# First two token tiles of the input projection taken singly, with the first weights loaded ahead of the second tile

## The chip, the cores and the metric

The kernel runs on one core of a Trainium2 chip. The metric is the device time of one execution in microseconds (us). Before the change it is 1400.34 us, the median of 3 runs (1399.54 to 1401.05).

## What is computed

One layer of an encoder on 1024 tokens of 1024 features, in float32: a norm, one wide input projection, two parallel branches, a merge, a feed-forward part and a final norm. The change touches the first lines of it alone:

```python
h = rmsnorm(x, norm_mix[l])          # x * rsqrt(mean(x*x) + EPS) * gain
proj = h @ w_in[l]
q, k, v, r, lr_f, lr_b, u, g_a, g_b = jnp.split(proj, split_points, axis=-1)
log_a_f = jax.nn.log_sigmoid(lr_f @ w_decay_up_fwd[l] + b_decay_fwd[l]) / GATE_NORMALIZER
...
o = o_fwd + o_bwd                    # gated linear attention, both directions, 4 heads
...
x = x + merged @ w_out[l]
x = x + (jax.nn.silu(gate) * up) @ w_ffn_out[l]
return rmsnorm(x, norm_final)
```

## The kernel before

**Numbers and tiles.** Every matrix product is made of three matmuls (`products`, line 288): each operand is split into a high part, rounded to the matmul's float32r format, and a low part, which is the rest. ScalarE (ACT in the profile) rounds, and VectorE (DVE) or GpSimd (POOL) subtracts. The tokens are cut into eight tiles of 128. `x` tiles arrive by DMA in four buffers that are used in turn, so that the load of tile t + 4 waits until tile t has been scaled (`load_x`, line 370; `norm_x`, line 393).

**The norm of one tile** (`norm_x`, lines 393 to 397, with lines 320 to 332) runs over three engines: ACT squares and sums the tile, DVE adds epsilon (the small `n1rs<-n1ms` row), POOL takes the power -1/2, and DVE multiplies the tile by it (`xn<-x,n1rs`). DVE takes its instructions in order, and so stands while POOL works on the power that its next instruction reads.

**The turn to features** (`to_features`, line 352). TensorE transposes the scaled tile into PSUM (`tr<-ident,xn`, line 338), ACT multiplies by the gain and rounds to the high part `hh` (line 345), and DVE makes the low part `hl` (line 348). Before the change this is always done for two token tiles at once: a PSUM bank holds two feature pieces of two token tiles, and an ACT or DVE instruction works on 128 partitions by 256 tokens.

**The first product** (`first_values`, line 415) multiplies one token tile by 288 columns: the 256 value columns of the first head and 32 columns of the low-rank decay inputs. It takes 8 features pieces of three matmuls each, 24 in all. The value columns come in four chunks of 256 KB (`raw`, line 206), the 32 decay columns in one small load (`lraw`, line 384). `FirstWeights` (line 236) splits them into `fwh` and `fwl`: the high part of a chunk on ACT, the low part of chunks 0 and 1 on DVE, of 2 and 3 on POOL; the decay columns wholly on POOL. When the sum of a token tile is done, ACT and DVE split it (`vh`, `vl`) and ACT copies the decay columns (`lr`, line 421), which on ACT stands behind the `vl` of DVE.

**The order of the work** is written out by hand: every engine executes what the program issues in the order in which it issues it. `begin` puts a generator on a side list, and `pump` (line 159), called after every three matmuls, takes its next step when a credit counted in matmul lengths has run out; `finish_side` runs what is left. In the first stage (lines 442 to 487) the order is: norm of tiles 0 and 1, their transposes, the split of all first weights, their gain and split, the norms of tiles 2 and 3, then pairs of token tiles; the norms of tiles t + 4 and t + 5 are begun ahead of tile t, the transposes for tiles t + 2 and t + 3 in the middle of tile t + 1.

Of the kernel before, what the change touches and what calls it, by code (L numbers as in the profile page):

```python
# [17 lines left out]
P = 128  # L18
# [34 lines left out]
def kernel(  # L53
# [146 lines left out]

    def load(src, kts, c0, width):
        per = min(HALF // width, kts)
        tiles = []
        for k0 in range(0, kts, per):
            raw = wts.tile([P, per, width], F32, tag="raw", name=name("raw"), bufs=4)
            nc.sync.dma_start(
                raw[:, :, :],
                src[k0 * P : (k0 + per) * P, c0 : c0 + width].rearrange("(k p) c -> p k c", p=P),
            )
            tiles.append(raw)  # L210
        return tiles

# [23 lines left out]
    class FirstWeights(Weights):  # L236
# [6 lines left out]

        def split_values(self, i, eng):
            split_to(*(t[:, :, :DV] for t in self.parts[i]), self.todo[i][:, :, :], eng)

# [81 lines left out]

    def norm_scale(xt, sq, s):
        ms = vec(1, s + "ms")  # L330
        nc.scalar.activation(sq[:, :], xt, AF.Square, scale=1.0 / 32.0, accum_out=ms[:, :])
        return rms_scale(ms[:, :], 1, s + "rs")

    def transpose_tile(ps, xt, i, kp):
# [16 lines left out]

    def to_features(xn, t0, act, gain):

        for kp in range(KT // 2):
            ps = bank(ps_g, "tr")
            for i in range(2):
                transpose_tile(ps, xn[i], i, kp)
            gain_and_split(ps, kp, t0, act, gain)
            yield 1

# [9 lines left out]
    def load_x(t):  # L370
        nc.sync.dma_start(xt[t % 4][:, :], x[t * P : (t + 1) * P, :])

    def load_rows(tile, at, v, n):
        nc.sync.dma_start(tile[at : at + n, :], v[0].rearrange("(j p) -> j p", p=P))
# [6 lines left out]
    load_rows(rows[0], 0, norm_mix, 8)  # L381
    load_x(1)
    first_raw = load(*next(order))
    nc.sync.dma_start(lraw[:, :, :], w_in[:, LR0:U0].rearrange("(k p) c -> p k c", p=P))
    for t in (2, 3):
        load_x(t)
# [5 lines left out]

    def norm_x(t):
        rs = norm_scale(xt[t % 4][:, :], xn[t % 4], "n1")
        scale_by(xn[t % 4], xt[t % 4][:, :], rs)
        if t + 4 < NT:
            load_x(t + 4)

    def norms(t0):
# [15 lines left out]
    def first_values(w, v, t):  # L415

        ps = bank(ps_mm)
        for kt in range(KT):
            mm3(ps[:, :VL], tokens(hT(kt, t // 4), t), w(kt), kt == 0, kt == KT - 1)
        split_to(*(part[:, t % 4, :] for part in v[t // 4]), ps[:, :DV])  # L420
        nc.scalar.copy(low_rows[:, t, :, :], ps[:, DV:VL].unsqueeze(1).broadcast_to([P, 4, 2 * RANK]))
# [33 lines left out]
    b_dec = (cols[1][:, 24:28], cols[1][:, 28:32])  # L455
    norm_x(1)
    trs = [bank(ps_g, "tr") for _ in range(KT // 2)]
    for t in range(2):
        for kp, ps in enumerate(trs):
            transpose_tile(ps, xn[t], t, kp)  # L460
    w = FirstWeights(first_raw, lraw)
    w.split_low()
    for i in range(KT // 2):
        w.split_values(i, nc.vector if i < 2 else nc.gpsimd)
    for kp, ps in enumerate(trs):
        gain_and_split(ps, kp, 0, hT, g_mix)
    norm_x(2)
    norm_x(3)
    for t in range(0, NT, 2):
        if t + 4 < NT:  # L470
            begin(norms(t + 4), 1)
        if t == 2:
# [3 lines left out]
            fetch()  # L476
        first_values(w, v, t)
        finish_side()
        if t == 0:
            vectors(1, 8)  # L480
        if t + 2 < NT:
            begin(to_features(xn[(t + 2) % 4 :], t + 2, hT, g_mix), 0.5)
        first_values(w, v, t + 1)
        finish_side()
# [1393 lines left out]
```

## Time and profile before

| what | value |
|---|---|
| time of the runs | 1400.34 us median, 1399.54 to 1401.05 |
| time of the profiled execution | 1400.29 us, of it 1398.6 us span |
| TensorE busy | 1367.3 us (98% of the span) |
| VectorE, ScalarE, GpSimd busy | 848.1, 624.0, 751.1 us |
| TensorE busy in the first 32 us | 22.76 us |

The span runs from the first to the last instruction of the profiled execution; the rest of its time, 1.7 us, lies around it. A row of the timeline has start, duration, engine, line, operation and tiles, how many instructions were merged in it, and in brackets how long the engine had stood idle before it and what ended that. A matmul's own duration overlaps that of the next, so its pace is read from the distance of two starts. PE is TensorE; SPq is the queue that issues the loads. Buffer numbers are left out of names, so `xn<-x` is the norm of any token tile.

### The profile page before, as it was taken

The numbers are of one execution on the slowest core, as the hardware profiler recorded it, in microseconds if no ns is written. First come the engines' busy times: TensorE is split into PE (matmuls) and PEld (weight loads), VectorE is DVE, ScalarE is ACT, GpSimd is POOL, SyncE is SP. The second block draws the span as 40 slices with busy tenths as digits, with TensorE's granted clock in tenths as the row PEclk, the third lists the DMA queues.
The fourth block names the chain that finished last, engine by engine and source line by source line (L and its number), as shares of the span: only waits on it lengthen the run. The fifth ranks groups of instructions, "written<-read, shape, count | busy, mean of one in ns | idle before, by whom it ended". The sixth has DMA issues, their size and how long they took to land. (4 is left out here: it accounts for less than half of the span.)

```text
span 1398.6 us, 18511 instructions
## 1 busy us (share of the span) xinstructions
PE 1367.3 (98%) x6654; PEld 1152.5 (82%) x6654; DVE 848.1 (61%) x1073; ACT 624.0 (45%) x1125; POOL 751.1 (54%) x565
## 2 busy tenths in 40 slices
PE   7999999999999999899999999999999999999997
PEld 6889898988888888788887888888888888888876
DVE  6266757667745885587875865556565556343364
ACT  6364655554334444455346633333333334453253
POOL 3261716041387555468665176666666667464364
PEclk9999999999999999999999999999999999999999
DMA  6211423322477668997425455554444447976461
GB/s 191 76 57 50 136 64 103 106 62 75 135 241 234 207 215 270 323 402 275 151 76 183 164 180 173 173 173 159 147 140 148 142 153 254 385 257 216 165 240 62
DMA packets 167453, 243.56 MB, mean 174 GB/s; under 512 B 10905, under 2 KB 97857, under 8 KB 167361
## 3 DMA queue, kind: packets, MB, share of 16 engines
q1 hardware_dynamic: 154944, 216.16, 46.3%
q10 hardware_dynamic: 12416, 26.22, 5.0%
q8 instruction: 52, 0.85, 0.3%
q14 instruction: 41, 0.33, 0.1%
HBM read 164.48 MB, written 77.86 MB: 173 GB/s over the span
## 5 line engine op out<-in xcount | busy, mean ns | idle before, releaser
L199 POOL TENSOR_TENSOR wl<-fs,wh 128x512 fp32r<-128x512 f32 x120 | 165.0, 1379 | 163.9 <-ACT wh L198 141.3
L291 PE MATMUL ps<-gl,wh 128*128 128x512 f32 x616 | 240.0, 390 | 0.8 <-DVE gl L1472 0.8
L291 PE MATMUL ps<-gh,wh 128*128 128x512 f32 x616 | 240.6, 391 | 0.0
L291 PE MATMUL ps<-gh,wl 128*128 128x512 f32 x616 | 239.9, 390 | 0.0
L199 POOL TENSOR_TENSOR wl<-fraw,wh 128x512 fp32r<-128x512 f32 x90 | 129.9, 1443 | 67.2 <-ACT wh L198 66.5
L199 POOL TENSOR_TENSOR ol<-gor,oh 128x1024 fp32r<-128x1024 f32 (+1 forms) x42 | 102.1, 2437 | 91.9 <-ACT oh L198 72.9
L291 PE MATMUL ps<-hh,wh 128*128 128x512 f32 x376 | 149.5, 398 | 0.0
L291 PE MATMUL ps<-hh,wl 128*128 128x512 f32 x376 | 146.8, 391 | 0.0
L291 PE MATMUL ps<-hl,wh 128*128 128x512 f32 x376 | 146.6, 390 | 0.0
L291 PEld LDWEIGHTS ps<-gl,wh 128*128 128x128 f32 x616 | 115.7, 188 | 24.9 <-DVE gl L1472 1.3
L291 PEld LDWEIGHTS ps<-gh,wl 128*128 128x128 f32 x616 | 115.7, 188 | 24.2
L199 POOL TENSOR_TENSOR wl<-raw,wh 128x512 fp32r<-128x512 f32 x44 | 61.4, 1411 | 137.7 <-ACT wh L198 135.2
L291 PEld LDWEIGHTS ps<-gh,wh 128*128 128x128 f32 x616 | 115.7, 188 | 23.6
L291 PE MATMUL ps<-oh,oh 128*128 128x512 f32 x308 | 120.0, 390 | 1.3 <-DVE x L1800 1.3
L291 PE MATMUL ps<-ol,oh 128*128 128x512 f32 x308 | 120.1, 390 | 0.2 <-DVE ol L199 0.2
L291 PE MATMUL ps<-oh,ol 128*128 128x512 f32 x308 | 119.9, 389 | 0.0
L199 POOL TENSOR_TENSOR wl<-wraw,wh 128x512 fp32r<-128x512 f32 x56 | 90.7, 1646 | 46.7 <-ACT wh L198 46.7
L199 DVE TENSOR_TENSOR ol<-wor,oh 128x1024 fp32r<-128x1024 f32 (+1 forms) x42 | 63.9, 1542 | 53.1 <-ACT oh L198 50.0
L198 ACT CAST wh<-fs 128x512 fp32r<-128x512 f32 x120 | 73.8, 615 | 30.8 <-DVE fs L902 23.1
L291 PEld LDWEIGHTS ps<-hh,wl 128*128 128x128 f32 x376 | 70.6, 188 | 15.1
L291 PEld LDWEIGHTS ps<-hl,wh 128*128 128x128 f32 x376 | 70.7, 188 | 13.4
L291 PEld LDWEIGHTS ps<-hh,wh 128*128 128x128 f32 x376 | 70.7, 188 | 13.4
(258 smaller groups left out, 3173.2 us busy)
## 6 DMA issues: line engine op xcount, KB each, us to landing
fraw<-in_w_ffn_in_dram SPq DMA_DIRECT2D x44, 512.0 KB, 6.4
gor<-g_out SPq DMA_DIRECT2D x35, 512.0 KB, 7.0
raw<-in_w_in_dram SPq DMA_DIRECT2D x48, 256.0 KB, 4.4
g_out<-s SPq DMA_DIRECT2D x44, 256.0 KB, 2.3
fraw<-in_w_in_dram SPq DMA_DIRECT2D x20, 512.0 KB, 4.2
wor<-t_out SPq DMA_DIRECT2D x20, 512.0 KB, 7.6
g_out<-g SPq DMA_DIRECT2D x33, 256.0 KB, 2.6
x<-in_x_dram SPq DMA_DIRECT2D x16, 512.0 KB, 3.9
```

Of the source, the lines that this page charges most:

```text
L198: nc.scalar.copy(hi, src)
L199: eng.tensor_tensor(lo, src, as_f32(hi), op=ALU.subtract)
L291: nc.tensor.matmul(ps, a[i], b[j], start=first and n == 0, stop=last and n == 2, skip_group_check=onto)
```

## The change

Loads: the first two weight chunks, the decay columns and the last two chunks are now issued ahead of `x` tile 1. Before, tile 1 stood ahead of them and the decay columns behind all four chunks.

Token tiles 0 and 1 are each turned to features by themselves (`features_of`): a PSUM bank holds two feature pieces of one token tile, and the ACT and DVE instructions work on 128 by 128. TensorE multiplies token tile 0 before it transposes token tile 1. The squares, roots and scalings of tiles 1, 2 and 3 are put one by one between the pieces of tiles 0 and 1. The high part of weight chunk 2 stands behind the first two pieces of tile 0 and its low part goes to DVE; chunk 3 is split wholly on POOL.

Tiles 2 and 3 are still turned to features together, with 256-token instructions, but now amid the matmuls of token tile 1, three matmuls apart. The norms of tiles 4 and 5, which stood ahead of the split of token tile 0's sum, stand behind the features of tiles 2 and 3. From the matmuls of token tile 2 on, every engine has the same instructions in the same order as before.

```diff
-    load_x(1)
-    first_raw = load(*next(order))
-    nc.sync.dma_start(lraw[:, :, :], w_in[:, LR0:U0].rearrange("(k p) c -> p k c", p=P))
-    for t in (2, 3):
+    first_raw = load(*next(order), and_then={1: load_low})
+    for t in (1, 2, 3):
         load_x(t)
...
-        def split_values(self, i, eng):
-            split_to(*(t[:, :, :DV] for t in self.parts[i]), self.todo[i][:, :, :], eng)
+        def high(self, i, copy=nc.scalar.copy):
+            copy(self.parts[i][0][:, :, :DV], self.todo[i][:, :, :])
+
+        def low_part(self, i, eng):
+            hi, lo = (t[:, :, :DV] for t in self.parts[i])
+            eng.tensor_tensor(lo, self.todo[i][:, :, :], as_f32(hi), op=ALU.subtract)
...
+    def square_x(t):
+        sums_of[t] = vec(1, "n1ms")
+        nc.scalar.activation(
+            xn[t % 4][:, :], xt[t % 4][:, :], AF.Square, scale=1.0 / 32.0, accum_out=sums_of[t][:, :]
+        )
+    def root_x(t):
+        scale_of[t] = rms_scale(sums_of.pop(t)[:, :], 1, "n1rs")
+    def scale_x(t):
+        scale_by(xn[t % 4], xt[t % 4][:, :], scale_of.pop(t))
+        if t + 4 < NT:
+            load_x(t + 4)
...
+    def split_values(v, t, ps):
         split_to(*(part[:, t % 4, :] for part in v[t // 4]), ps[:, :DV])
         nc.scalar.copy(low_rows[:, t, :, :], ps[:, DV:VL].unsqueeze(1).broadcast_to([P, 4, 2 * RANK]))
...
-    norm_x(1)
-    trs = [bank(ps_g, "tr") for _ in range(KT // 2)]
-    for t in range(2):
-        for kp, ps in enumerate(trs):
-            transpose_tile(ps, xn[t], t, kp)
     w = FirstWeights(first_raw, lraw)
     w.split_low()
-    for i in range(KT // 2):
-        w.split_values(i, nc.vector if i < 2 else nc.gpsimd)
-    for kp, ps in enumerate(trs):
-        gain_and_split(ps, kp, 0, hT, g_mix)
-    norm_x(2)
-    norm_x(3)
-    for t in range(0, NT, 2):
+    for i in range(2):
+        w.high(i)
+        w.low_part(i, nc.vector)
+    def features_of(t, *between):
+        trs = [bank(ps_g, "tr") for _ in range(KT // 2)]
+        for k in range(KT):
+            c = slice(k % 2 * P, (k % 2 + 1) * P)
+            nc.tensor.transpose(trs[k // 2][:, c], xn[t][:, k * P : (k + 1) * P], ident[:, :])
+        cols = slice(t * P, (t + 1) * P)
+        for kp, ps in enumerate(trs):
+            pair = [(*hT(k, 0), ps[:, k % 2 * P : (k % 2 + 1) * P], g_mix[:, k : k + 1]) for k in (2 * kp, 2 * kp + 1)]
+            for hi, _, src, g in pair:
+                nc.scalar.activation(hi[:, cols], src, AF.Copy, scale=g)
+            for hi, lo, src, g in pair:
+                nc.vector.scalar_tensor_tensor(
+                    lo[:, cols], src, g, as_f32(hi[:, cols]), op0=ALU.mult, op1=ALU.subtract
+                )
+            for step in between[kp]:
+                step()
+    features_of(
+        0, (), (
+            partial(w.high, 2), partial(w.low_part, 2, nc.vector), partial(w.high, 3, nc.gpsimd.tensor_copy),
+            partial(w.low_part, 3, nc.gpsimd), partial(square_x, 1), partial(root_x, 1),
+        ), (partial(scale_x, 1),), (partial(square_x, 2), partial(root_x, 2)),
+    )
+    ps = first_values(w, v, 0)
+    features_of(
+        1, (), (partial(scale_x, 2), partial(square_x, 3), partial(root_x, 3)), (), (partial(scale_x, 3),)
+    )
+    split_values(v, 0, ps)
+    begin(to_features(xn[2:], 2, hT, g_mix, 0.6), 1.8)
+    begin(norms(4), 0)
+    ps = first_values(w, v, 1)
+    finish_side()
+    split_values(v, 1, ps)
+    vectors(1, 8)
+    for t in range(2, NT, 2):
```

Three places show what moves. In the names, `xn_5` is the buffer of token tiles 0 and 4, `xn_6` of 1 and 5, `xn_7` of 2 and 6, `xn_8` of 3 and 7.

ScalarE in the changed kernel, from the high part of the second weight chunk to the square of tile 3:

```order
L246 CAST fwh_27_179<-raw_12_142 128x2x256
L493 ACTIVATE hh_37_209<-tr_33_197,cols8_173 128x128 x2
L493 ACTIVATE hh_39_215<-tr_34_198,cols8_173 128x128 x2
L246 CAST fwh_29_181<-raw_13_145 128x2x256
L398 ACTIVATE xn_6_131,n1ms_41_225<-x_2_127 128x1024
L493 ACTIVATE hh_43_230<-tr_35_199,cols8_173 128x128 x2
L493 ACTIVATE hh_45_238<-tr_36_200,cols8_173 128x128 x2
L398 ACTIVATE xn_7_132,n1ms_47_244<-x_3_128 128x1024
L493 ACTIVATE hh_37_209<-tr_50_274,cols8_173 128x128 x2
L493 ACTIVATE hh_39_215<-tr_51_275,cols8_173 128x128 x2
L398 ACTIVATE xn_8_133,n1ms_54_296<-x_4_129 128x1024
```

The square of tile 1 (`xn_6`), which waits for that tile's load, now stands ahead of the last four pieces of tile 0; before, all squares of tiles 0 and 1 stood ahead of the weights, and those of tiles 2 to 5 behind all pieces of tiles 0 and 1.

VectorE before, from the norm of tile 3 to the features of tiles 2 and 3:

```order
L327 TENSOR_SCALAR xn_8_133<-x_4_129,n1rs_50_261 128x1024
L322 TENSOR_SCALAR n1rs_53_275<-n1ms_52_273 128x1
L327 TENSOR_SCALAR xn_5_130<-x_1_126,n1rs_53_275 128x1024
L322 TENSOR_SCALAR n1rs_55_293<-n1ms_54_291 128x1
L327 TENSOR_SCALAR xn_6_131<-x_2_127,n1rs_55_293 128x1024
L199 TENSOR_TENSOR vl_19_162<-ps_51_266,vh_18_161 128x256
L450 COPY cols32_174<-vps_24_172 128x32
L348 SCALAR_TENSOR_TENSOR hl_40_229<-tr_57_312,cols8_173,hh_39_228 128x256 x2
```

VectorE in the changed kernel, from the scaling of tile 3 to the split of token tile 1's sum:

```order
L332 TENSOR_SCALAR xn_8_133<-x_4_129,n1rs_55_298 128x1024
L199 TENSOR_TENSOR vl_19_162<-ps_49_249,vh_18_161 128x256
L348 SCALAR_TENSOR_TENSOR hl_38_210<-tr_57_327,cols8_173,hh_37_209 128x256 x2
L348 SCALAR_TENSOR_TENSOR hl_40_216<-tr_58_339,cols8_173,hh_39_215 128x256 x2
L348 SCALAR_TENSOR_TENSOR hl_44_231<-tr_59_351,cols8_173,hh_43_230 128x256 x2
L348 SCALAR_TENSOR_TENSOR hl_46_239<-tr_60_363,cols8_173,hh_45_238 128x256 x2
L327 TENSOR_SCALAR n1rs_62_377<-n1ms_61_375 128x1
L332 TENSOR_SCALAR xn_5_130<-x_1_126,n1rs_62_377 128x1024
L327 TENSOR_SCALAR n1rs_64_383<-n1ms_63_381 128x1
L332 TENSOR_SCALAR xn_6_131<-x_2_127,n1rs_64_383 128x1024
L199 TENSOR_TENSOR vl_19_162<-ps_56_314,vh_18_161 128x256
```

The norms of tiles 4 and 5 have moved from ahead of `vl` of token tile 0 to behind the features of tiles 2 and 3, ahead of `vl` of token tile 1.

SyncE in the changed kernel, the first loads:

```order
L371 DMA x_1_126<-in_x_dram 128x1024
L377 DMA rows_134<-in_norm_mix_dram 8x128
L206 DMA raw_11_140<-in_w_in_dram 128x2x256
L206 DMA raw_12_142<-in_w_in_dram 128x2x256
L374 DMA lraw_10_137<-in_w_in_dram 128x8x32
L206 DMA raw_13_145<-in_w_in_dram 128x2x256
L206 DMA raw_14_147<-in_w_in_dram 128x2x256
L371 DMA x_2_127<-in_x_dram 128x1024
```

The load of `x` tile 1 (`x_2`) has moved from the third place to the eighth; the seven larger loads among the eight are the same ones as before.

More of the change, by code (lines that the diff above doesn't have):

```diff
@@ L199, in split_to, with load @@
         eng.tensor_tensor(lo, src, as_f32(hi), op=ALU.subtract)
-    def load(src, kts, c0, width):
+    def load(src, kts, c0, width, and_then={}):
         per = min(HALF // width, kts)
@@ L210, in load @@
             tiles.append(raw)
+            and_then.get(len(tiles) - 1, bool)()
         return tiles
@@ L327, in scale_by @@
         nc.vector.tensor_scalar(dst[:, :], src, rs[:, :], None, op0=ALU.mult)
[L329 to L332, printed above, removed]
     def transpose_tile(ps, xt, i, kp):
@@ L350, in gain_and_split, with to_features @@
             )
-    def to_features(xn, t0, act, gain):
+    def to_features(xn, t0, act, gain, every=1):
         for kp in range(KT // 2):
@@ L358, in to_features @@
             gain_and_split(ps, kp, t0, act, gain)
-            yield 1
+            yield every
     xt = [slot(shape=(D,), s="x") for _ in range(4)]
@@ L371, in load_x, with load_low @@
         nc.sync.dma_start(xt[t % 4][:, :], x[t * P : (t + 1) * P, :])
+    def load_low():
+        nc.sync.dma_start(lraw[:, :, :], w_in[:, LR0:U0].rearrange("(k p) c -> p k c", p=P))
     def load_rows(tile, at, v, n):
@@ L391, with norm_x @@
     hT = Activations("h")
-    def norm_x(t):
-        rs = norm_scale(xt[t % 4][:, :], xn[t % 4], "n1")
-        scale_by(xn[t % 4], xt[t % 4][:, :], rs)
+    sums_of = {}
+    def square_x(t):
[3 more added lines that the diff above has]
+        )
+    scale_of = {}
+    def root_x(t):
+        scale_of[t] = rms_scale(sums_of.pop(t)[:, :], 1, "n1rs")
+    def scale_x(t):
+        scale_by(xn[t % 4], xt[t % 4][:, :], scale_of.pop(t))
         if t + 4 < NT:
             load_x(t + 4)
+    def norm_x(t):
+        square_x(t)
+        root_x(t)
+        scale_x(t)
     def norms(t0):
@@ L419, in first_values @@
             mm3(ps[:, :VL], tokens(hT(kt, t // 4), t), w(kt), kt == 0, kt == KT - 1)
+        return ps
+    def split_values(v, t, ps):
         split_to(*(part[:, t % 4, :] for part in v[t // 4]), ps[:, :DV])
@@ L476 @@
             fetch()
-        first_values(w, v, t)
+        split_values(v, t, first_values(w, v, t))
         finish_side()
-        if t == 0:
-            vectors(1, 8)
         if t + 2 < NT:
             begin(to_features(xn[(t + 2) % 4 :], t + 2, hT, g_mix), 0.5)
-        first_values(w, v, t + 1)
+        split_values(v, t + 1, first_values(w, v, t + 1))
         finish_side()
```

## The prediction

> **What bounds the kernel now.** I read the page first, then the stretches of busy time, then the timelines of TensorE, ScalarE, VectorE and GpSimd over the first 32 us, with the waits.
>
> ```profile
> span 1398.6 us, 18511 instructions
> 0.00:32.00 32.00, 22.76 (x147) 20.91 (x148) 18.51 (x45) 20.07 (x45) 11.84 (x55) 1.00 0.68 209
> 32.00:60.00 28.00, 27.65 (x173) 25.31 (x174) 11.18 (x24) 14.06 (x35) 5.63 (x4) 1.00 0.26 75
> 60.00:1398.00 1338.00, 1316.85 (x6336) 1106.31 (x6335) 818.37 (x1004) 589.84 (x1047) 733.68 (x506) 1.00 0.52 175
> ```
>
> The columns behind the length are the busy time of PE, PEld, DVE, ACT and POOL, the granted clock, the DMA share and GB/s. From 60 us on PE is busy 1316.85 of 1338 us, in an order that the change leaves alone; so what the change is worth is how much sooner or later PE comes out of the first 32 us, where it stands 9.2 us. This is PE there:
>
> ```profile
> 7.29 1.97 PE L338 MATMUL tr<-ident,xn 128*128 128x128 f32 x8 [2.32 <-DVE xn L327]
> 10.18 1.97 PE L338 MATMUL tr<-ident,xn 128*128 128x128 f32 x8 [0.92 <-DVE xn L327]
> 11.80 0.59 PE L291 MATMUL ps<-fwh,hh 128*128 128x288 f32 x1
> 13.28 0.44 PE L291 MATMUL ps<-fwl,hh 128*128 128x288 f32 x1
> 13.52 0.44 PE L291 MATMUL ps<-fwh,hl 128*128 128x288 f32 x1
> 14.58 0.29 PE L291 MATMUL ps<-fwh,hl 128*128 128x288 f32 x1
> 14.71 0.30 PE L291 MATMUL ps<-fwh,hh 128*128 128x288 f32 x1
> 18.52 0.44 PE L338 MATMUL tr<-ident,xn 128*128 128x128 f32 x2 [0.87 <-DVE n1rs L322]
> 26.80 0.60 PE L338 MATMUL tr<-ident,xn 128*128 128x128 f32 x4
> 27.16 0.38 PE L291 MATMUL ps<-fwh,hh 128*128 128x288 f32 x1
> 31.87 0.40 PE L291 MATMUL ps<-fwh,hh 128*128 128x288 f32 x1 [0.34 <-ACT hh L345]
> 32.75 0.40 PE L291 MATMUL ps<-fwh,hl 128*128 128x288 f32 x1 [0.35 <-DVE hl L348]
> ```
>
> PE starts its first product at 11.80, at a pace of 0.24 us a matmul, which becomes 0.13 near 14.0 us. At 31.87, the first matmul of token tile 4, it still waits, for `hh`. That is the marker: from there on it waits for nothing up to 60 us (27.65 busy of 28.00, the rest in this wait and the next, 0.35 for `hl`). What ends late there is on ACT and DVE:
>
> ```profile
> 7.36 1.06 ACT L331 ACTIVATE xn<-x 128x1024 f32<-128x1024 f32 x1 [1.80 <-DMA x<-in_x_dram]
> 10.53 0.62 ACT L198 CAST fwh<-raw 128x512 fp32r<-128x512 f32 x1 [0.28 <-DMA raw<-in_w_in_dram]
> 11.06 3.02 ACT L345 ACTIVATE hh<-tr,cols 128x256 fp32r<-128x256 f32 x8
> 13.92 1.10 ACT L331 ACTIVATE xn<-x 128x1024 f32<-128x1024 f32 x1
> 21.79 0.27 ACT L421 COPY lr<-ps 128x128 f32<-128x128 f32 x1 [3.30 <-DVE vl L199]
> 21.95 3.03 ACT L345 ACTIVATE hh<-tr,cols 128x256 fp32r<-128x256 f32 x8
> 31.18 0.27 ACT L421 COPY lr<-ps 128x128 f32<-128x128 f32 x1 [2.15 <-DVE vl L199]
> 31.34 3.03 ACT L345 ACTIVATE hh<-tr,cols 128x256 fp32r<-128x256 f32 x8
> ```
> ```profile
> 16.23 0.75 DVE L327 TENSOR_SCALAR xn<-x,n1rs 128x1024 f32<-128x1024 f32 x1 [0.92 <-POOL n1rs L323]
> 17.71 0.75 DVE L327 TENSOR_SCALAR xn<-x,n1rs 128x1024 f32<-128x1024 f32 x1 [0.67 <-POOL n1rs L323]
> 20.66 0.75 DVE L327 TENSOR_SCALAR xn<-x,n1rs 128x1024 f32<-128x1024 f32 x1 [0.66 <-POOL n1rs L323]
> 21.33 0.42 DVE L199 TENSOR_TENSOR vl<-ps,vh 128x256 fp32r<-128x256 f32 x1
> 22.83 3.23 DVE L348 SCALAR_TENSOR_TENSOR hl<-tr,cols,hh 128x256 fp32r<-128x256 f32 x8 [0.98 <-ACT hh L345]
> 30.05 0.75 DVE L327 TENSOR_SCALAR xn<-x,n1rs 128x1024 f32<-128x1024 f32 x1 [0.66 <-POOL n1rs L323]
> ```
>
> Read back from 31.34: `hh` stands behind `lr`, that behind `vl`, that on DVE behind the norm of tile 7 (30.05), and so on back to the features of tiles 2 and 3 (21.95, 22.83), the norms of tiles 2 to 5 (16.23 to 20.66) and the features of tiles 0 and 1 (11.06), which began when the last weight chunk had landed (10.53). It is one chain on ACT, DVE and POOL from 10.5 to 31.9 us. A norm costs it (20.66 - 16.23) / 3 = 1.48 us, of which 0.66 is DVE standing while POOL takes the power.
>
> **The change part by part.** *Loads.* `x` tile 0 lands at 4.41 as before (first row below).
>
> ```profile
> 4.41 1.06 ACT L331 ACTIVATE xn<-x 128x1024 f32<-128x1024 f32 x1 [2.32 <-DMA x<-in_x_dram]
> 11.29 0.77 POOL L249 CAST fwh<-lraw 128x64 fp32r<-128x64 f32 x4 [1.96 <-DMA lraw<-in_w_in_dram]
> 12.02 1.16 POOL L251 TENSOR_TENSOR fwl<-lraw,fwh 128x64 fp32r<-128x64 f32 x4
> 13.13 2.55 POOL L199 TENSOR_TENSOR fwl<-raw,fwh 128x512 fp32r<-128x512 f32 x2
> ```
>
> The 512 KB of `x` tile 1 landed 2.95 us later (7.36), so two chunks, also 512 KB, land by 7.4; the decay columns took 11.29 - 10.53 = 0.76, so they land at 8.1; chunks 2 and 3 at (10.53 - 7.36) / 4 = 0.79 each, at 8.9 and 9.7. `x` tile 1 is now the last of the same seven loads that before were all in at 11.29: that is its upper end. At the chunks' pace, 3.17 us a megabyte, it would be in at 4.41 + 1.625 x 3.17 = 9.6: the lower end. Neither is nearer, so I take 10.5.
>
> *First product.* The transposes of tile 0 take (11.80 - 10.18) / 8 = 0.2 each and end near 8.9; POOL has the first high and low decay columns 0.73 + 0.32 behind 8.1. So PE starts the product of tile 0 at about 9.0, 2.8 us sooner.
>
> *Smaller pieces.* ACT and DVE do 16 pieces of 128 tokens in place of 8 of 256. These rows give what a piece costs beside its length:
>
> ```profile
> L198 ACT CAST fwh<-raw 128x512 fp32r<-128x512 f32 x4 | 2.4, 614 | 0.4 <-DMA raw<-in_w_in_dram 0.3
> L198 ACT CAST vh<-ps 128x256 fp32r<-128x256 f32 x8 | 3.1, 390 | 0.9 <-PE ps L291 0.9
> L199 DVE TENSOR_TENSOR fwl<-raw,fwh 128x512 fp32r<-128x512 f32 x2 | 1.3, 686 | 0.0
> L199 DVE TENSOR_TENSOR vl<-ps,vh 128x256 fp32r<-128x256 f32 x8 | 3.4, 420 | 2.7 <-ACT vh L198 2.7
> ```
>
> 128 elements less save 0.11 on ACT ((614 - 390) / 2) and 0.13 on DVE ((686 - 420) / 2). From 0.37 (3.02 / 8) and 0.40 (3.23 / 8) a piece remain about 0.25 and 0.27; the ends are half of the long piece, 0.19 and 0.20, and 0.29 and 0.31. So 16 pieces cost 4.0 against 3.0 on ACT, 4.3 against 3.2 on DVE: a whole microsecond more on each engine. [...]
>
> *Up to the features of tiles 2 and 3.* ACT squares tile 1 from 10.5 to 11.55, then does the last four pieces of tile 0 (1.0) to 12.6. DVE ends the last `hl` of tile 0 near 13.8, behind the scaling of tile 1. PE, at 0.24 a matmul from 9.0 to 14.0 and 0.13 after that, ends tile 0 at about 14.5 and the transposes of tile 1 (26.80 to 27.16 for four, so 0.7 for eight) at 15.2, the first bank at 14.8. ACT then has four pieces, the square of tile 3 and four pieces, 1.0 + 1.04 + 1.0, from about 14.9 to 18.0; DVE has eight pieces and two scalings of 0.7 behind it, up to about 19.3; then `vl`, and ACT's `lr`. So `hh` of tiles 2 and 3 starts at about 19.9 to 20.0, against 21.95: **2.0 us gained** up to here. The square of tile 2 and the roots are hidden in PE's cold matmuls.
>
> *Behind them.* Before, from the `hh` of tiles 2 and 3 (21.95) to that of tiles 4 and 5 (31.34) it took 9.39. The same work stands there now, and in addition the norms of tiles 4 and 5, which DVE had done ahead: 2 x 1.48 = **2.96 paid back**. PE's wait for tile 3 amid tile 1 (its transposes now stand ahead of the last 12 matmuls) and for tile 5 amid tile 3 cost nothing of their own, being inside this chain.
>
> Sum: 2.96 - 2.0 = about +1.0 at the marker, PE at 32.9. If the pace doubles earlier than at 14.0, tile 0 ends with its last `hl` and the sum falls to about +0.4. I take the middle, **+0.7**. The profiled execution took 1400.29, its span of 1398.6 and 1.7 around it, and stands at the runs' median of 1400.34; so **1401.0**. With the ends of all terms: an early clock (+0.4), 16 short pieces on the one chain (16 x 0.06 = 1.0 less) and tile 1 in at 9.6 (0.9 less) give -1.5; the clock as now (+1.0), 16 long pieces (16 x 0.04 = 0.6 more) and tile 1 in at 11.3 (0.8 later, of which PE's cold matmuls hide 0.5) give +1.9. A measurement of this kernel can tell about 0.2% from no change, 2.8 us; both ends lie within.
>
> **The rivals.** *The early start survives* (faster). If PE kept its 2.8 us, and the waits of 0.87, 0.34 and 0.35 went too, the time would be 1400.3 - 4.4 = 1395.9. For it: PE has more busy time in these 32 us than any other engine. Against: `lr` waits 3.30 and 2.15 for `vl`, and DVE stands for POOL in each norm; nothing in the change shortens a norm. Chance 0.08.
>
> *`x` tile 1 comes late* (slower). The square of tile 1 stands on ACT ahead of half of tile 0's pieces; DVE's `hl`, PE's last 12 matmuls and the norms queue behind. From 11.3 on, each microsecond of lateness is one on the chain; with it in at 11.3 the sum is 1.0 + 0.3 = +1.3, so past a landing at 12.8 (+1.5 more) it leaves the 0.2%. Landing where the next tile does, before its square at 13.92, would give about 1400.3 + 1.3 + 2.6 = 1404.2. POOL's split of chunk 3, a subtraction of 2.55 / 2 = 1.3 and a copy that I bound by the same 1.3, starts when POOL is done with the decay columns (8.1 + 0.73 + 1.16 = 10.0) and ends by 12.6; the root of tile 1, due near 11.9, is at worst 0.7 late, mostly behind PE's cold matmuls. Against: the seven loads are the same. Chance 0.09.
>
> *The clock stays half longer.* The pace changed at 14.0 though the granted clock of the row reads 1.00, and transposes from 7.29 on had not raised it. If it rises only after the transposes of tile 1, the last three matmuls of tile 0 take 0.3 more and the transposes of the first bank 0.2; what is slow behind them hides in PE's wait for tile 3. That is 1.0 + 0.5 = +1.5, 1401.8. [...] Chance 0.13, inside 0.2%.
>
> The forecast with its bounds has the remaining 0.70.
>
> **How the numbers follow.** Likeliest: the chain, 1401.0. The ends of the sum are 1398.8 and 1402.2. The runs lie up to 0.8 from their median (1399.54 to 1401.05), so the range goes 0.2 below the lower end, a corner where three terms are at their best, and 0.7 above the upper, where the clock and a moderately late `x` tile 1 add up: 1398.6 to 1402.9. Outside are the first two rivals and little else. Faster by over 0.2%: 0.08; slower: 0.09; within: 0.83.
>
> **What would show it.** Right: the first matmul of 288 columns near 9; `hh` of tiles 2 and 3 near 20; two norms, 2.96 us, on DVE between those features and `vl`; the first matmul of token tile 4 between 31 and 34. Wrong: that matmul before 30 or past 35; a square of tile 1 that starts after 12; pieces over 0.35 us; DVE no longer standing for POOL's power; or a difference that grows after 60 us, where no order changed.

## The result, and the profile after

The changed kernel takes 1403.58 us (median of 15 runs, 1401.43 to 1405.87), the kernel before in the same comparison 1400.79 (15 runs, 1398.68 to 1402.73): ratio 1.0020, 95% interval 1.0012 to 1.0028. It is slower by about 2.8 us. Forecast were 1401.0 and a range to 1402.9: the sign of the sum was right, its size too small. The profiled execution was the fastest of the 15, 1401.43 us with a span of 1399.7.

First the stretches of busy time, as before (PE, PEld, DVE, ACT, POOL, granted clock, DMA share, GB/s):

```profile
0.00:32.00 32.00, 21.81 (x144) 20.34 (x145) 19.36 (x53) 20.46 (x49) 12.53 (x55) 1.00 0.66 209
32.00:60.00 28.00, 26.36 (x169) 24.09 (x168) 12.21 (x26) 13.99 (x35) 5.64 (x4) 1.00 0.24 72
60.00:1398.00 1338.00, 1319.09 (x6345) 1107.51 (x6343) 812.52 (x1004) 590.47 (x1048) 732.12 (x506) 1.00 0.52 175
```

PE starts its products earlier and still does less by 32 us: 21.81 us of work where it had done 22.76. Behind 32 us it now stands 1.64 us, where it stood 0.35. The timeline of PE shows where:

```profile
9.10 0.59 PE L296 MATMUL ps<-fwh,hh 128*128 128x288 f32 x1
...
12.09 0.41 PE L296 MATMUL ps<-fwh,hl 128*128 128x288 f32 x1
12.33 0.31 PE L296 MATMUL ps<-fwh,hh 128*128 128x288 f32 x1
12.48 0.30 PE L296 MATMUL ps<-fwl,hh 128*128 128x288 f32 x1
...
14.31 0.40 PE L296 MATMUL ps<-fwh,hl 128*128 128x288 f32 x1 [0.74 <-DVE hl L495]
...
19.93 0.44 PE L338 MATMUL tr<-ident,xn 128*128 128x128 f32 x2 [1.63 <-DVE xn L332]
...
20.61 0.60 PE L338 MATMUL tr<-ident,xn 128*128 128x128 f32 x4
...
21.45 0.60 PE L338 MATMUL tr<-ident,xn 128*128 128x128 f32 x4
...
27.93 0.44 PE L338 MATMUL tr<-ident,xn 128*128 128x128 f32 x2 [0.47 <-DVE xn L332]
...
33.76 0.40 PE L296 MATMUL ps<-fwh,hh 128*128 128x288 f32 x1 [1.29 <-ACT hh L345]
...
34.65 0.40 PE L296 MATMUL ps<-fwh,hl 128*128 128x288 f32 x1 [0.35 <-DVE hl L348]
```

The first product starts at 9.10, 2.70 us sooner. The pace changes from 0.24 to about 0.13 a matmul at 12.33. Then four waits eat the lead, and the marker, the first matmul of token tile 4, stands at 33.76 against 31.87: 1.89 us later. ACT and DVE:

```profile
8.21 1.14 ACT L493 ACTIVATE hh<-tr,cols 128x128 fp32r<-128x128 f32 x4 [0.84 <-PE tr L488]
...
10.27 1.06 ACT L398 ACTIVATE xn<-x 128x1024 f32<-128x1024 f32 x1 [0.42 <-DMA x<-in_x_dram]
...
15.36 1.14 ACT L493 ACTIVATE hh<-tr,cols 128x128 fp32r<-128x128 f32 x4 [1.88 <-PE tr L488]
...
20.24 0.27 ACT L442 COPY lr<-ps 128x128 f32<-128x128 f32 x1 [1.41 <-DVE vl L199]
20.41 3.35 ACT L345 ACTIVATE hh<-tr,cols 128x256 fp32r<-128x256 f32 x8
23.65 1.06 ACT L398 ACTIVATE xn<-x 128x1024 f32<-128x1024 f32 x1
...
28.24 0.27 ACT L442 COPY lr<-ps 128x128 f32<-128x128 f32 x1 [2.15 <-DVE vl L199]
...
33.23 1.94 ACT L345 ACTIVATE hh<-tr,cols 128x256 fp32r<-128x256 f32 x5
```
```profile
11.45 0.15 DVE L327 TENSOR_SCALAR n1rs<-n1ms 128x1 f32<-128x1 f32 x1 [0.86 <-ACT xn L398]
...
13.24 0.75 DVE L332 TENSOR_SCALAR xn<-x,n1rs 128x1024 f32<-128x1024 f32 x1 [0.67 <-POOL n1rs L328]
13.91 0.60 DVE L495 SCALAR_TENSOR_TENSOR hl<-tr,cols,hh 128x128 fp32r<-128x128 f32 x2
...
24.82 0.15 DVE L327 TENSOR_SCALAR n1rs<-n1ms 128x1 f32<-128x1 f32 x1 [0.16 <-ACT xn L398]
25.64 0.75 DVE L332 TENSOR_SCALAR xn<-x,n1rs 128x1024 f32<-128x1024 f32 x1 [0.66 <-POOL n1rs L328]
...
27.12 0.76 DVE L332 TENSOR_SCALAR xn<-x,n1rs 128x1024 f32<-128x1024 f32 x1 [0.66 <-POOL n1rs L328]
27.79 0.42 DVE L199 TENSOR_TENSOR vl<-ps,vh 128x256 fp32r<-128x256 f32 x1
```

`hh` of tiles 2 and 3 starts at 20.41, 1.54 us sooner than before (21.95). From there to `hh` of tiles 4 and 5 it takes 33.23 - 20.41 = 12.82, where it took 9.39: 3.43 us paid back. The two norms stand on DVE between the features and `vl` (25.64, 27.12), each with its 0.66 for POOL's power, and `lr` on ACT stands 2.15 for that `vl`. And POOL:

```profile
9.15 1.62 POOL L256 TENSOR_TENSOR fwl<-lraw,fwh 128x64 fp32r<-128x64 f32 x4
10.72 0.61 POOL L246 CAST fwh<-raw 128x512 fp32r<-128x512 f32 x1
11.40 1.29 POOL L250 TENSOR_TENSOR fwl<-raw,fwh 128x512 fp32r<-128x512 f32 x1
12.65 0.56 POOL L328 TENSOR_TENSOR n1rs<-n1rs,half_neg 128x1 f32<-128x1 f32 x1
```

The root of tile 1 runs at 12.65, right behind the subtraction of chunk 3, though its sum was ready at 11.6 (11.45 + 0.15 on DVE).

### The profile page after: what moved, and what is told of

Read it like the earlier page. It is cut to its first block, busy times and chain, and to the rows that moved or that the text cites. A ratio compares the mean times of both kernels' runs of the same rounds, so it can differ in the third digit from the quotient of the medians.

```text
span 1399.7 us, 18525 instructions
## 1 busy us (share of the span) xinstructions
PE 1367.3 (98%) x6654; PEld 1151.9 (82%) x6654; DVE 844.1 (60%) x1082; ACT 624.9 (45%) x1132; POOL 750.3 (54%) x565
## 4 chain that ended last, share of the span: by engine, by line
PE 65%; DVE 5%; issue 3%; POOL 3%; DMA 2%; ACT 2%; ACTq 0%; POOLq 0%; DVEq 0%; SPq 0%
PE ps L296 63%; POOL wl L199 1%; DMA u_out<-uph 1%; DVE res L1818 1%; PE tp L1039 1%; DMA wor<-t_out 0%; DMA ph<-p_out 0%; PE op L880 0%; DVE x L1603 0%; DVE fs L949 0%; PE yb L296 0%; POOL n3rs L1586 0%; DVE ws L1099 0%; DMA u_out<-upl 0%; ACT wh L198 0%
```

## Experiments

The theory after this: the head, up to the marker, is one chain on ACT, DVE and POOL; the change shortens its first part by less than forecast and lengthens its second part by more. Two things were open: whether the 2.8 us between the medians, against 1.9 at the marker and 1.1 at the end of the two profiled executions, arise in the head at all; and whether something about the clock adds to it.

**The kernel before against itself** (no edit).

> The kernel before, unchanged, against itself. Every theory: ratio 1.000, first matmul of token tile 4 at 31.9 us, medians within 0.8 us of each other. What it is for: the profiled execution of the changed kernel is 1.1 us longer than that of the kernel before, the medians differ by 2.8. Theory A (the clock): other executions of the changed kernel hold more half-rate stretches of 3.4 us than its profiled one, those of the kernel before do not; then the mean granted clock of the runs here is 0.998 in most, against 0.994 to 0.998 (mostly 0.996 and 0.997) in the 15 runs of the changed kernel. Theory B (the clock has no part): the clocks here spread like those of the changed kernel, 0.996 or 0.997 in most.

1400.71 us (11 runs) against 1400.92, ratio 1.000 (0.9991 to 1.0009). The mean clocks are 0.996 to 0.999, on average 0.9971, and 0.9966 in the 32 runs beside it; those of the changed kernel were 0.9963. They spread alike, so theory A does not explain the difference of the whole kernels. But the first matmul of tile 4 was at 31.29, not 31.9. This is ACT (start, duration):

```profile
7.58 2.13 ACT L198 CAST fwh<-raw 128x512 fp32r<-128x512 f32 x3
9.98 0.62 ACT L198 CAST fwh<-raw 128x512 fp32r<-128x512 f32 x1 [0.28 <-DMA raw<-in_w_in_dram]
10.51 3.02 ACT L345 ACTIVATE hh<-tr,cols 128x256 fp32r<-128x256 f32 x8
...
21.36 3.03 ACT L345 ACTIVATE hh<-tr,cols 128x256 fp32r<-128x256 f32 x8
```

The last weight chunk was there at 9.98, where the prediction's profile had it at 10.53; everything behind it is 0.55 to 0.6 us earlier. PE was at full pace from 10.7 in this execution and from 14.1 in the other, which moved nothing but its own slack.

**The root ahead of chunk 3's subtraction.**

```diff
-            partial(w.low_part, 3, nc.gpsimd), partial(square_x, 1), partial(root_x, 1),
+            partial(square_x, 1), partial(root_x, 1), partial(w.low_part, 3, nc.gpsimd),
```

> The changed kernel, with the root of tile 1 on GpSimd ahead of the subtraction of weight chunk 3. Theory (GpSimd's queue): the root ran at 12.65, a microsecond behind its sum, because the subtraction (11.40 to 12.69) stood ahead of it; ahead of it, it runs at 11.6, tile 1 is scaled at 12.6 in place of 13.24, the last hl of tile 0 at 13.2 in place of 13.91, hh of tiles 2 and 3 at 19.9 in place of 20.41, and the first matmul of token tile 4 at 33.2 in place of 33.76: 0.5 us. Rival (covered): PE then waits for the low part of chunk 3, which ends near 13.5, and hh of tiles 2 and 3 stays at 20.4, tile 4 at 33.8.

`hh` of tiles 2 and 3 came at 20.57, the marker at 33.92, the median was 1404.17 (ratio 1.0023, 1.0014 to 1.0032): nothing gained, as the rival had it, but not for its reason. On POOL and DVE:

```profile
11.79 0.56 POOL L328 TENSOR_TENSOR n1rs<-n1rs,half_neg 128x1 f32<-128x1 f32 x1 [0.53 <-DVE n1rs L327]
12.32 1.28 POOL L250 TENSOR_TENSOR fwl<-raw,fwh 128x512 fp32r<-128x512 f32 x1
```
```profile
12.59 1.56 DVE L332 TENSOR_SCALAR xn<-x,n1rs 128x1024 f32<-128x1024 f32 x1
```

The root came early and the scaling started at 12.59, as the theory said; but beside POOL's subtraction it took 1.56 us in place of 0.75, and so ended at 14.15, where it had ended at 13.99.

**The two norms back ahead of `vl` of tile 0.**

```diff
+    for _ in norms(4):
+        pass
     split_values(v, 0, ps)
     begin(to_features(xn[2:], 2, hT, g_mix, 0.6), 1.8)
-    begin(norms(4), 0)
```

> The changed kernel, with the norms of tiles 4 and 5 ahead of vl of tile 0 and so ahead of the features of tiles 2 and 3, where they stood before the change. Theory (one chain on ACT, DVE and POOL, in which a norm costs the same wherever it stands): hh of tiles 2 and 3 starts at about 23.0 in place of 20.41, hh of tiles 4 and 5 at 33.0 in place of 33.23, and the first matmul of token tile 4 at 33.5 in place of 33.76; the median stays within 0.5 us of the changed kernel's, 1403.6. Rival (before the change the two norms lay under PE's slow matmuls, and the change uncovered them): the first matmul of token tile 4 comes at about 31 and the median at about 1400.5.

In the trace the theory is right: `hh` of tiles 2 and 3 at 23.32, of tiles 4 and 5 at 32.78, the marker at 33.31. The two norms cost the chain 2.91 us ahead of the features (23.32 against 20.41) and 3.36 behind them (12.82 against 32.78 - 23.32 = 9.46): nearly the same, so it was not a cover that was lost. The median, however, was the rival's, 1401.04 (ratio 1.0005, 0.9996 to 1.0013). This contradiction is taken up below.

**The norms taken apart.** The squares of tiles 4 and 5 go between `vh` and `lr` of tile 0, where ACT stood 1.41 us, those of 6 and 7 between `vh` and `lr` of tile 1; their roots behind `vl`; the scalings behind `vl` of tile 1.

```diff
-        split_to(*(part[:, t % 4, :] for part in v[t // 4]), ps[:, :DV])
+        hi, lo = (part[:, t % 4, :] for part in v[t // 4])
+        nc.scalar.copy(hi, ps[:, :DV])
+        for u in squares:
+            square_x(u)
+        nc.vector.tensor_tensor(lo, ps[:, :DV], as_f32(hi), op=ALU.subtract)
+        for u in squares:
+            root_x(u)
...
-    split_values(v, 1, ps)
+    split_values(v, 1, ps, (6, 7))
+    for t in (4, 5, 6, 7):
+        scale_x(t)
```

> The changed kernel with the norms of tiles 4 to 7 taken apart: the squares of 4 and 5 on ACT between vh and lr of tile 0, where ACT stood for 1.41 us, the squares of 6 and 7 likewise in tile 1 (2.15), the roots behind vl, and the four scalings on DVE behind vl of tile 1, with the roots done long before. Theory (DVE's and ACT's waits inside the norms are the price that is paid back, 4 times 0.66 for POOL's power, and 1.04 for each pair's first square): hh of tiles 2 and 3 starts at 21.1 in place of 20.41, hh of tiles 4 and 5 near 30, and the first matmul of token tile 4 at about 31.5 (31.0 to 32.3) in place of 33.76; the median is about 2.2 us below the changed kernel's 1403.6. Rival (PE's own work from its first matmul on sets the end): the first matmul of token tile 4 stays at 33.3 or later.

`hh` of tiles 4 and 5 started at 29.66 in place of 33.23, and the marker came at 32.14 with no wait at it or in the matmuls behind it, so that from there on PE was 2.3 us ahead of the changed kernel; the median was 1398.72, with runs from 1396.95 to 1403.22. Against the kernel before a gain is not shown: the ratio over all runs is 0.9992 (0.9983 to 1.0001). From `hh` of tiles 2 and 3 (20.73) to that of tiles 4 and 5 it took 8.93 us in place of 12.82, with the same norms, whose four scalings still take 2.74 on DVE: what was paid back is mostly waiting between the steps of a norm, and not the steps themselves.

**The head alone.** Executions of the whole kernel spread over 4 us. So the kernels were cut behind the products of token tile 7; what comes behind is left out.

```diff
+    nc.sync.dma_start(out[:P, :], as_f32(v[1][1][:, :, :]).rearrange("p t c -> p (t c)"))
+    return
```

> The kernel before, cut off behind the products of token tile 7 (it then stores one tile and ends; everything behind is left out), so that its time is that of the head alone, in many executions and not only in the profiled one. Every theory: about 50 us; it is the yardstick for the three cut kernels beside it.

> The changed kernel, cut off at the same place. Theory A (the head is 1.9 us longer in every execution, as the profiled one shows at the first matmul of token tile 4, and the rest of the 2.8 us between the medians comes from behind the head): its median is 1.9 us, within 0.4, above that of the cut kernel before. Theory B (the profiled execution had a short head; the whole difference arises in the head): 2.8 us above.

> The changed kernel with the norms of tiles 4 and 5 ahead of vl of tile 0, cut off at the same place. Its profile had the first matmul of token tile 4 at 33.31, 0.45 us before the changed kernel's 33.76, but its median was 2.5 us lower. Theory A: here it is 0.45 us, within 0.3, below the cut changed kernel; the other 2 us came from behind the head. Theory B: 2.5 us below.

| cut kernel | median us (runs) | lowest to highest |
|---|---|---|
| before | 52.96 (4) | 52.88 to 53.52 |
| changed | 55.38 (6) | 55.10 to 56.76 |
| changed, norms first | 54.91 (5) | 54.58 to 55.05 |

The changed head is 2.42 us longer, between the two theories; norms first is 0.47 below it, so theory A holds there. The profile of the cut kernel before has `hh` of tiles 0 and 1 at 10.20 and the marker at 31.05, 2.37 ahead of the cut changed kernel's 33.42. In this profile and the one with 31.29 the head before is 0.6 to 0.8 shorter than in the profile from which the forecast was made, which makes the difference between 1.9 and 2.4. Four of the six executions of the cut changed kernel lie at 55.10 to 55.39, two at 56.74 and 56.76; the median of the four is 55.26, 2.30 above the cut kernel before. One of the two long ones is the profiled one (PE; the pace is the distance of two starts):

```profile
33.42 0.40 PE L296 MATMUL ps<-fwh,hh 128*128 128x288 f32 x1 [1.30 <-ACT hh L345]
33.66 0.29 PE L296 MATMUL ps<-fwl,hh 128*128 128x288 f32 x1
34.30 0.40 PE L296 MATMUL ps<-fwh,hl 128*128 128x288 f32 x1 [0.35 <-DVE hl L348]
...
35.08 0.29 PE L296 MATMUL ps<-fwl,hh 128*128 128x288 f32 x1
35.21 0.35 PE L296 MATMUL ps<-fwh,hl 128*128 128x288 f32 x1
35.35 0.45 PE L296 MATMUL ps<-fwh,hh 128*128 128x288 f32 x1
35.59 0.45 PE L296 MATMUL ps<-fwl,hh 128*128 128x288 f32 x1
...
38.71 0.31 PE L296 MATMUL ps<-fwh,hl 128*128 128x288 f32 x1
38.86 0.29 PE L296 MATMUL ps<-fwh,hh 128*128 128x288 f32 x1
```
```profile
35.31:38.72 3.41, 3.41 (x17) 3.41 (x16) 2.01 (x6) 1.14 (x4) 0.00 (x0) 0.50 0.00 0
```

From 35.31 to 38.72 the granted clock is 0.50 (third value from the end) and a matmul takes 0.24 in place of 0.13: 14 of them cost 1.5 us.

**The pieces of 128 tokens alone**, in the kernel before with its loads, cut. The first attempt made both tiles' pieces bank by bank, the second all of tile 0 and then all of tile 1:

```diff
-    for kp, ps in enumerate(trs):
-        gain_and_split(ps, kp, 0, hT, g_mix)
+    for i in range(2):
+        for kp, ps in enumerate(trs):
+            gain_and_split(ps, kp, 0, hT, g_mix, i)
```

> The kernel before with nothing changed but the features of tiles 0 and 1 made in 16 pieces of 128 tokens on each engine in place of 8 of 256, cut off at the same place. Theory (the price of the pieces is on the chain, 0.25 against 0.37 on ACT, 0.27 against 0.40 on DVE): ACT's pieces take 4.0 us in place of 3.0, hh of tiles 2 and 3 comes 1.0 us later, and the median is 1.0 us above that of the cut kernel before. Rival (hidden under PE's slow matmuls of tiles 0 and 1): within 0.3 us of it.

57.97 us, 5.0 above the cut kernel before, a miss of both: ACT waited 0.68 for `hl` ahead of every group of four pieces, PE stood up to 2.00 us at a time, and the clock was at half for 6.8 us in a row (matmuls 0.24 apart from 22.87 to 26.37). It measures that order and not the pieces.

> The kernel before, with the features of tiles 0 and 1 in pieces of 128 tokens, all of tile 0 and then all of tile 1 (the first attempt at this alternated the two tiles within each bank and made ACT wait for DVE piece by piece), cut off behind the products of tile 7. Theory (the pieces' price is on the chain): hh of tiles 2 and 3 1.0 us later than in the cut kernel before, 22.1 in place of 21.12, and the median about 53.9 in place of 52.96. Rival (hidden under PE's cold matmuls): 53.0 to 53.2.

53.52 us (6 runs, 53.37 to 54.69), 0.56 above. From the first `hh` to that of tiles 2 and 3 (cut kernel, ACT):

```profile
9.91 4.24 ACT L348 ACTIVATE hh<-tr,cols 128x128 fp32r<-128x128 f32 x16
...
21.76 3.04 ACT L348 ACTIVATE hh<-tr,cols 128x256 fp32r<-128x256 f32 x8
```

11.85 us, against 21.12 - 10.20 = 10.92 in the cut kernel before and 10.85 and 10.89 in the whole ones: 0.93 on the chain, where the prediction had a microsecond. The earlier first piece (9.91) is why the median shows less.

**The norms taken apart, cut; chunk 3 off GpSimd, cut; both and more, cut.** The second puts chunk 3's high part on ACT and its low part on DVE, which stood there 0.86 us; the third adds to the first two the square of tile 3 ahead of the pieces of tile 1, and moves the scalings of tiles 2 and 3 up.

```diff
-            partial(w.high, 2), partial(w.low_part, 2, nc.vector), partial(w.high, 3, nc.gpsimd.tensor_copy),
-            partial(w.low_part, 3, nc.gpsimd), partial(square_x, 1), partial(root_x, 1),
-        ), (partial(scale_x, 1),), (partial(square_x, 2), partial(root_x, 2)),
+            partial(w.high, 2), partial(w.low_part, 2, nc.vector), partial(w.high, 3),
+            partial(w.low_part, 3, nc.vector), partial(square_x, 1), partial(root_x, 1),
+        ), (partial(scale_x, 1),), (partial(square_x, 2), partial(root_x, 2), partial(square_x, 3), partial(scale_x, 2)),
...
-        1, (), (partial(scale_x, 2), partial(square_x, 3), partial(root_x, 3)), (), (partial(scale_x, 3),)
+        1, (partial(root_x, 3),), (partial(scale_x, 3),), (), ()
```

> The changed kernel with the norms of tiles 4 to 7 taken apart (squares while ACT stands for vl, roots behind vl, scalings behind vl of tile 1), cut off behind the products of tile 7. In the whole kernel it left no wait of PE at token tile 4, where the changed kernel has 1.29 and 0.35 us; in the cut changed kernel two of six executions took 56.7 us and four 55.1 to 55.4, and the profile of one of the two long ones shows half the clock for 3.4 us right behind that wait. Theory A (the norms behind the features of tiles 2 and 3 are the price, and the wait that they open is what the clock answers): median about 53.1 (from 52.8 to 53.4), and no execution more than 0.8 us above the fastest. Theory B (the half-rate stretch has nothing to do with this wait): about one execution in three still lies 1.3 us or more above the others.

> The changed kernel with weight chunk 3 taken off GpSimd (its high part on ACT behind that of chunk 2, its low part on DVE, which stood for 0.86 us there), cut off behind the products of tile 7. With the root of tile 1 merely ahead of the subtraction PE waited for chunk 3 instead and nothing was gained; here neither is late. Theory (GpSimd's queue held tile 1, 0.65 us): the square of tile 1 starts 0.2 later, its scaling at 12.7 in place of 13.24, the last hl of tile 0 0.5 earlier, hh of tiles 2 and 3 near 19.6 in place of 20.05 to 20.41, and the median is 0.5 us below the cut changed kernel's 55.38. Rival (PE's cold matmuls set the end of tile 0): the median stays within 0.2 us.

> The norms taken apart and chunk 3 off GpSimd, and the square of tile 3 on ACT ahead of the pieces of tile 1, where ACT stood for 1.88 us, with the scalings of tiles 2 and 3 moved up on DVE, cut off behind the products of tile 7. Theory (the three were the price; each comes off the chain): hh of tiles 2 and 3 at about 19.5, no wait of PE for the scaling of tile 3 (1.63 us before), the median 51.8 (51.2 to 52.5), a microsecond below the cut kernel before, 52.96. Rival (with the norms taken apart PE is the bound, and the sooner features only lengthen its waits): within 0.3 us of the cut kernel with the norms taken apart alone.

| cut kernel | median us (runs) | lowest to highest |
|---|---|---|
| norms taken apart | 53.01 (4) | 52.95 to 53.19 |
| chunk 3 off GpSimd | 55.88 (6) | 55.03 to 56.99 |
| both, and the square of tile 3 | 52.06 (4) | 51.84 to 52.27 |

The first and the third come out as their theories had them, 2.37 and 3.32 us below the cut changed kernel. The second gained 0.37 in the trace (`hh` of tiles 2 and 3 at 19.68 against 20.05, the marker at 33.03 against 33.42), near the forecast 0.5, but its times don't show it. Three of its six executions took 56.28 to 56.99, and the median of the other three is 55.21, 0.05 below the 55.26 of the changed kernel. Single times are too rough for 0.4 us here, for the closing store varies too: from the start of the last matmul to the end of the span it took 5.58 us in this profile (48.17 to 53.75) and 4.96 in that of the cut changed kernel (50.07 to 55.03). (What its expectation says of the root moved ahead isn't in that trace: PE stood there 0.41 for `hl`, not for chunk 3.)

It still has the waits of 1.29 and 0.36 at tile 4. Taken together, 5 of 12 executions of the two cut kernels with that wait are 1.25 to 1.96 us above the fastest of their kernel, and none of 17 of the four cut kernels (before, norms first, taken apart, both) in which PE stands there 0.42 at a time at most. The mean granted clocks fit: 0.944 to 0.969 in the five, and 0.973 to 1.000 in all but two (0.968 and 0.969) of the other 24; half the clock for 3.41 us takes 0.03 off such a mean (3.41 x 0.5 / 55.0). Not every long execution is of this kind. The cut kernel with the pieces tile by tile, in which PE stands 0.57 and 1.04 near 17 and 18 us, has two of six, 0.95 and 1.32 above its fastest, with clocks of 0.994 and 0.975, and its others have 0.941 to 0.990: what made these two long isn't known.

**The whole kernels again.**

> The changed kernel, unchanged, again. Theory (the head decides: 2.2 to 2.4 us in most executions, 3.8 in about one of three, where PE's wait at token tile 4 brings half the clock for 3.4 us; behind the head the kernels are alike): median 2.2 to 3.2 us above the kernel before, a profile with the first matmul of token tile 4 at 33.4 to 33.9 us. Rival (the 2.8 us of the first comparison were a matter of that chip): below 1.5 us.

1403.28 us (11 runs) against 1400.80 (30 runs), ratio 1.0020 (1.0011 to 1.0029), marker at 33.89: as the theory had it.

> The changed kernel with the norms of tiles 4 and 5 ahead of vl of tile 0, again. Cut off behind tile 7 it was 1.95 us above the cut kernel before, but in the whole kernel the median was only 0.1 us above it (interval of the ratio 0.9996 to 1.0013). Theory (behind the head the kernels are alike, and the first median was low by chance): 1.0 to 2.3 us above the kernel before. Rival (the rest of the kernel takes back what this head loses): within 0.5 us of it again.

1401.65 us, the median 0.85 above; the ratio over all runs is 1.0011 (1.0002 to 1.0020), which is 0.3 to 2.8 us. The two measurements together allow its head's 1.95 us only at the edge. The contradiction is softer and not gone.

> The kernel before, with three squares of 128x512, about 1.9 us, added on ACT ahead of hh of tiles 4 and 5 (their results are not used); nothing else is moved, so that PE waits there about 2.2 us in place of 0.3 to 0.4. Theory (a wait of PE at this place costs its length, and in part of the executions 1.5 us of half clock behind it; nothing later gives it back): the first matmul of token tile 4 at about 33.2 and the median 1.9 to 3.4 us above the kernel before. Rival (stalls behind the head, the one near 577 us above all, give back what the head loses): the same shift at the head, and a median less than 1.2 us above.

```diff
+        if t == 2:
+            spare = t2(s="spare")
+            for _ in range(3):
+                nc.scalar.activation(spare[:, :], xt[3][:, :HALF], AF.Square, scale=1.0 / 32.0)
```

PE in the old kernel with nothing but that wait added:

```profile
33.04 0.40 PE L291 MATMUL ps<-fwh,hh 128*128 128x288 f32 x1 [2.21 <-ACT hh L345]
```

The marker moved from 31.29 to 33.04, and the median is 1403.49, 2.7 above (ratio 1.0022, 1.0012 to 1.0032): more than the 1.75 of the marker, and within the theory's 1.9 to 3.4. A wait at this place alone makes the old kernel as slow as the changed one, and nothing behind gives it back: the theory.

> The whole kernel with the norms of tiles 4 to 7 taken apart, chunk 3 off GpSimd and the square of tile 3 ahead of the pieces of tile 1; cut off behind tile 7 it took 52.06 us against 52.96 of the cut kernel before. Theory (the head decides): median 0.9 us below the kernel before, and 1.5 at most, as PE no longer waits at token tile 4: about 1400.0. Rival (the rest gives back or takes more, as the first whole runs with the norms taken apart, 2.2 us below at an equal head, suggest): more than 2 us below, or not below at all.

1398.05 us (11 runs) against 1400.80, ratio 0.9981 (0.9971 to 0.9990): it beats both kernels. ACT and what is left of PE's waits in the head:

```profile
14.69 2.17 ACT L499 ACTIVATE hh<-tr,cols 128x128 fp32r<-128x128 f32 x8
19.19 3.11 ACT L345 ACTIVATE hh<-tr,cols 128x256 fp32r<-128x256 f32 x8
28.12 3.12 ACT L345 ACTIVATE hh<-tr,cols 128x256 fp32r<-128x256 f32 x8
```
```profile
25.65 0.41 PE L338 MATMUL tr<-ident,xn 128*128 128x128 f32 x2 [0.85 <-DVE xn L332]
26.23 0.44 PE L338 MATMUL tr<-ident,xn 128*128 128x128 f32 x2 [0.16 <-DVE xn L332]
```

It gains 2.7 us where its head gains 0.9: more than the theory's 1.5, so the rival's part of the statement, that the rest adds its own, holds here.

**What stays open.** Behind the marker all these kernels have the same instructions in the same order on every engine, yet the profiled executions do not keep the distance that they have there. The main place is a wait for ACT near 577 us. PE restarts there at 577.82 before and at 578.40 after (waits of 3.77 and 2.12), so that 1.3 of the 1.9 us vanish in these two executions; in two others with the changed kernel's shift (33.92, 33.89) PE restarts at 579.46 and 579.32, and 0.4 and 0.5 vanish.

In eight of the ten whole profiles the clock falls to half at the end of this wait or behind it (granted 0.50 from 577.29 to 580.70 before and from 578.95 to 582.36 in the changed kernel). In the two of norms first, with waits of 2.31 and 1.75, it does not, and PE, followed matmul by matmul against the first profile of the kernel before, wins 1.3 us there. But these two have their stretch of half clock near 231 us instead, behind waits of 1.78 and 1.76, and lose 0.7 to 0.9 with it; seven other profiles have a wait of 1.72 to 1.78 there and keep the clock. Both end 0.8 us before the first profile of the kernel before and 0.1 behind its second. The last version is 2.0 ahead of the first of these profiles at 60 us and 1.4 ahead of the second, more than the 0.9 of the cut kernels, so a part of its 2.7 may lie in how the loads fell. How often each of this happens in the executions that weren't profiled isn't known, and so neither why norms first loses less than its head, nor why the last version gains more.

## Why the prediction was wrong

**What held.** The head bounds, and as one chain: two norms cost about the same ahead of the features and behind, 2.91 and 3.36. `x` tile 1 was in at 10.27 (forecast 10.5), the first product began at 9.10 (9.0). The 16 pieces of 128 tokens took 4.24 in a row on ACT, 0.26 apiece (forecast 0.25), and on the chain they cost 0.93 (1.0). DVE stands 0.66 for POOL's power in the moved norms. The rivals did not come: the early start was lost within the head, tile 1 was not late, and the clock rose at 12.3, not after 14. One reading beside the third rival, that transposes had not raised the clock, holds for its profile alone: in the second profile of the kernel before PE was at full pace from 10.7, with nothing but transposes behind it (7.57 on), and the first product, at 11.12, took 0.37 at once, where it took 0.59 in the first. There, too, PE had been at work since the transposes of tile 1 at 10.18, 3.8 us ahead of the change of pace at 14.0.

**The step that failed is the sum of the path, in four terms, each too small in the same direction.**

1. "`hh` of tiles 2 and 3 starts at about 19.9 to 20.0": it was 20.41, so 1.54 were gained and not 2.0. The root of tile 1, "at worst 0.7 late, mostly behind PE's cold matmuls", was a microsecond late and not hidden: PE was at full pace from 12.33 and stood 0.74 for the last `hl` behind tile 1's scaling (13.24), so that tile 0 ended at 14.95 and not at 14.5. Taking chunk 3 off GpSimd brought 0.37 back in a trace; the times of that run don't show it.
2. "2.96 paid back": it was 3.43. The same eight `hh` took 3.35 in place of 3.03, because PE does three matmuls between two banks (transposes at 20.61 and 21.45, 0.84 apart), and DVE waited 0.16 for the square of tile 4, which stands behind them. The prediction held the waits amid tiles 1 and 3 to cost nothing of their own and overlooked the pace.
3. The early clock was to take 0.6 off the sum, half of which was counted. The clock was early, and took off nothing, since tile 0 ended with the late `hl`: 0.3.
4. The baseline. The one profile of before had its last weight chunk at 10.53; five other executions of the same loads had it at 9.38 to 10.05, with markers of 31.29 and 31.05 in the two where nothing else was changed. The square of `x` tile 1, which is loaded ahead of the chunks, began at 7.36 in the one and at 5.93 to 6.93 in the five. The chain started 0.5 to 1.1 too late in the profile from which the 2.0 were counted.

0.7 + 0.46 + 0.47 + 0.3 = 1.9 us, the distance of the two first profiles at the marker; with 0.6 for the baseline 2.5, against 2.3 to 2.4 measured in the cut kernels and 2.5 to 2.8 in the whole ones. The first three terms are read from one trace, and the pace in the second was not tried by itself. The range took up the clock, the pieces and tile 1 at their ends, but not the scatter of the loads in the baseline nor a root that PE does not hide.

**What was not thought of** is that half the clock can follow a wait of PE at the marker: it did in one profile of the cut kernel, where it cost 1.5 us, and the long executions, 5 of 12 with such a wait against 0 of 17 without, 1.25 to 1.96 us above the fastest, and their clocks are in line with it. It does not always: in the five other profiles with such a wait, the one of the kernel before with 2.21 us added among them, the clock stays full there. What decides it wasn't shown. In the whole kernels the mean clocks don't tell the two apart (0.9963 and 0.9972 after, 0.9966 to 0.9971 before), so what it adds there stays open.

## What to carry to other kernels

Work that one engine starts sooner is worth only what the chain behind it keeps: here 2.7 us at PE's first product became a loss of 2.4 at token tile 4, because the chain behind it gave back a part at once and each moved norm carried a wait for another engine's small step into the path; taken apart, with squares in ACT's gaps and the roots done before DVE needs them, the same start beats the old kernel, by 0.9 us in the head and 2.7 in the whole. A term of under a microsecond asks for more than one profile of the baseline, since one late load moved the whole chain by 0.6; and a kernel cut off behind the disputed stage measures it to some tenths of a microsecond where executions of the whole kernel spread over 4, if the few long ones are looked at by themselves. When an instruction is taken out of a queue, look at what will run beside it then.

## What the hardware showed that was not expected

- A scaling of 128x1024 on DVE took 0.75 us alone (changed kernel, 13.24) and 1.56 beside a 128x512 subtraction on POOL (the root ahead of chunk 3's subtraction, 12.59). It was no accident of that run: two scalings of a later norm (`n3rs`) run beside such subtractions in each of the ten whole profiles and take 1.74 and about 1.81 us (before, DVE and POOL below), and none of the other 203 of this shape in all profiles took over 0.76. Four casts of 128x64 on POOL took 0.77 before and 1.66 in the changed kernel, at another time beside other work.

```profile
762.83 1.74 DVE L327 TENSOR_SCALAR xn<-x,n3rs 128x1024 f32<-128x1024 f32 x1 [0.66 <-POOL n3rs L1539]
```
```profile
762.76 1.26 POOL L199 TENSOR_TENSOR wl<-fraw,wh 128x512 fp32r<-128x512 f32 x1
```

- The granted clock fell to 0.50 for 3.41 us (35.31 to 38.72 in the cut changed kernel) a microsecond behind a PE wait of 1.30 and one of 0.35, and in most whole profiles at the wait near 577 us (again for 3.41, with waits of 3.77 before and 2.12 in the changed kernel); behind a wait of 1.6 near 765 us in the same profiles (1.61 and 1.62 in these two) it did not. The length of the wait does not tell the cases apart: the first profile of the changed kernel has nearly the same two waits at the marker, 1.29 and 0.35, the kernel before with the added squares has 2.21 and 0.35, and neither is followed by half the clock.
